# Word transposes through transfers into float32r tiles, in a hybrid attention and retention block

## The chip, the cores and the metric

The kernel runs on one core of a Trainium2 chip. The metric is the device time of one execution in microseconds; of several runs the median counts. A profile is one more execution of the same program, recorded instruction by instruction. Its engines are PE (TensorE; its weight loads are listed apart as PEld), DVE (VectorE), ACT (ScalarE), POOL (GpSimd) and SP (SyncE, which here issues nearly all DMA transfers).

## The reference

One decoder block on `x` of 512 tokens and 1024 channels, all in float32:

```python
h = rms_norm(x, norm_pre)
proj = h @ w_in                       # 6936 columns, split into 15 parts
# mixer A: 8 query heads of 64, 2 key/value groups
#   compressed branch: blocks of 32 tokens, stride 16, through a small MLP -> 31 keys and values
#   selected branch and window branch: at 512 tokens both cover all earlier tokens
o = g0 * o_c + g1 * o_s + g2 * o_w    # g = sigmoid(g_n + b), one per head and branch
y_a = (o * silu(z_n)) @ w_nsa_o
# mixer B: retention, 4 heads, key width 128, value width 256, chunks of 128 tokens
att = einsum(q_chunk, k_chunk) * decay_mask
o = att @ v_chunk + (q_chunk * q_dec) @ R_prev      # R: state carried from chunk to chunk
y_b = (group_norm(o) * silu(z_r)) @ w_ret_o
merged = sigmoid(m_a) * y_a + sigmoid(m_b) * y_b
return x + rms_norm(merged @ w_out, norm_post)
```

There are at most 16 selected blocks of 64 tokens and only 8 blocks in 512 tokens, so the selection leaves no block out.

## The kernel before

**Two types of four bytes.** `FT` is float32, `FR` is float32r, a type of the same size on which TensorE makes one pass over rounded operands. To keep float32's precision the kernel splits a word into a rounded high part and a remainder, both FR (`act` or `cp_any` for the high part, `sub_split` for the remainder), and multiplies in three parts: high by high, high by low, low by high (`mm3`). A transpose also runs on TensorE (`tr`, line 226). Of a float32 tile ("a word transpose") it goes against `ident` in float32; the result in PSUM is the whole word, which is split only then. Only the queries are split first and transposed as FR, against `identr`. The type of a tile is that of the arena it lies in, `arena_f` (42 KB a partition) or `arena_r` (70 KB); `at(kb, n, dt)` cuts a tile out by its address.

**Stages.** The weights come as one stream in the order of their use, 512 KB a transfer (two k tiles of 128 x 512), into one of `NR = 4` raw tiles. `splitter` and `split_lo` make `whi` and `wlo` of each half, nine such pairs ahead (`NW = 9`). `main` is the chain of projections on TensorE: A (compressed and selected keys and values), C (window keys and values, gate row), Q, two compression layers, and then the blocks of `PLAN`: Z, MA, ZR 0, QK 0, VR 0, ZR 1, QK 1, VR 1, MB, NO, RO and so on, with the output projection last. Each block fills two accumulators in turn; a tail for each tile (`tail_a`, `tail_c`, `tail_q`, `tail_qk`, `ret`, ...) takes it out of PSUM and goes on with it.

**Where words are transposed.** `tail_a` and `tail_c` rotate the keys, copy them to doubled columns on DVE (`doubled`, line 511) and transpose them (`keysT`, two transposes a tile; the raw keys and values of the compressed branch, four more). `att_cmp` computes the compressed branch's probabilities and transposes eight tiles of them for each query tile. `att_head` makes the probabilities of one head: two matmuls, mask and maximum on DVE (line 790), exponential on ACT, scaling by gate / sum on DVE or ACT, whichever the planner expects to be done first. `att_block` transposes one key block of the four heads of a group (four transposes to a PSUM bank), splits it into `ph` and `pl` (a `PHL` tile) and adds its product with the values to the group's output bank with two matmuls of 512 columns (`av`). `att_sum` ends a group of a query tile; when all eight are done, it loads the retention's mask `dm` and hands tiles and banks on to retention. `tail_qk` transposes retention's rotated queries and keys (four a tile), `ret` the gated, normalised outputs (four a tile). The norm's row (`rs`) and the compression layers' hidden tiles are transposed as well.

**Buffers.** Rings hand out tiles: `PR` 8 probability tiles (four heads a unit), `PHL` 3, `NAT` 4 tiles of 512 words for tails, `KD6` and `KD2` the doubled keys, `GB` 2, `VR` retention's values, `SMC` 1 for the compressed branch.

**What sets the order.** The class `Order` is a planner: all tails and stages are generators, it runs them against a model of each engine's time, and writes each engine's instructions in the order in which it let them go. `main` has the lowest rank (`MAIN = 9`), attention heads 3, their units 2, most tails 1. So each engine's queue, SP's included, is fixed when the program is built; on the chip an instruction waits for its semaphores, and what stands behind it on its engine waits too. The planner charges a float32 transpose 107 ns and an FR one 58, and 100 and 85 ns for going into float32 on TensorE and back:

```python
    def tr(ps, a, idn, r=0.0):
        T.transpose(ps, a, idn)
        return od.pe(58 if a.dtype == FR else 107, r, a.dtype == FT)
```

Dependencies that decide around the change: `ret` may take the first value tiles out of their accumulators when the attention of query tiles 2 and 3 is done and there is a `VR` tile, the later ones and all further steps when all attention is done; block QK 1 needs the outputs of the first half of retention; NO waits for `ga_split`, which waits for all of retention; RO needs `gbh` and `gbl`, written at the end of `ret`.

Of the kernel before, what the change touches and what calls it, by code (L numbers as in the profile page):

```python
# [27 lines left out]
NR, NW = 4, 9  # L28
# [109 lines left out]
def block_kernel(ctx: ExitStack, tc, x, xT, g_pre, ws, small, w2s, norm_post, rope_r, dmask, out):  # L138
# [5 lines left out]
    cp.tile([P, 48], FT, name="pad")  # L144
# [3 lines left out]
    rp = ctx.enter_context(tc.tile_pool(name="raw", bufs=1))  # L148
    pp = ctx.enter_context(tc.tile_pool(name="ps", bufs=1, space=PSUM))
# [83 lines left out]

    def sub_split(lo, src, hi, r, e="dve"):
        return tt(lo, src, f(hi), OP.subtract, r, e)
# [18 lines left out]
    PHL = Ring([at(o, 1024, FR) for o in (60, 64, 40)])  # L254
# [20 lines left out]
    KD6 = Ring([at(32 + 3 * i, 768) for i in range(2)])  # L275
    KD2 = Ring([at(8 + i, 256) for i in range(2)])
    NAT = Ring([bp.tile([P, 512], FT, name=f"nat{i}") for i in range(4)])
    PR = Ring([at(8 + 2 * i, 512) for i in range(8)])
# [4 lines left out]
    GB = Ring([at(16 + 2 * i, 512) for i in range(2)])  # L283
# [195 lines left out]
    gate = cp.tile([P, NT, 24], FT, name="gate")  # L479
    kc = cp.tile([P, 2, 2, 32], FR, name="kc")  # L480
    vcs = cp.tile([96, 2, 2, 64], FR, name="vcs")
# [26 lines left out]
    def doubled(kn, a, b, kd, r):  # L508

        n = (b - a) // 64  # L510
        V.tensor_copy(kd.rearrange("p (a r c) -> p a r c", a=n, r=2),  # L511
                      kn[:, a:b].rearrange("p (a c) -> p a c", c=64).unsqueeze(2).broadcast_to([P, n, 2, 64]))
        return od.op("dve", 0.53 * n * P + 70, r, True)

    def keysT(kd, off, br, t, r):
        ps = yield from PT.get()
        yield r + PE_LAG
        for g in range(2):
            e = tr(ps[:, g * P:(g + 1) * P], kd[:, off + g * P:off + (g + 1) * P], ident, r)
# [16 lines left out]
    def tail_a(t, ps, e, ring):  # L536
# [8 lines left out]
        kd = yield from KD6.get()  # L545
        e = doubled(kn, 0, 384, kd, e)
        ev = vals(kn[:, 384:512], 0, t, 0.0)
        NAT.put(kn, ev)
        yield from keysT(kd, 512, 0, t, e)
        pc = yield from PT.get()  # L550
        yield e + PE_LAG
        for i in range(4):
            ep = tr(pc[:, i * P:(i + 1) * P], kd[:, i * P:(i + 1) * P], ident, e)
        KD6.put(kd, ep)
# [13 lines left out]
    def tail_c(t, ps, e):  # L568
# [7 lines left out]
        kd = yield from KD2.get()  # L576
        e = doubled(kn, 0, 128, kd, e)
        ev = vals(kn[:, 128:256], 1, t, 0.0)
        NAT.put(kn, ev)
        e = yield from keysT(kd, 0, 1, t, e)  # L580
        KD2.put(kd, e)
# [139 lines left out]
    def av(t, g, st, mv, r):  # L721
        a = avs[t, g]
        e = mm(a["po"], st, mv, a["n"] == 0, a["n"] == a["total"] - 1, r)
        a["n"] += 1
        a["e"] = e
        return e

    def att_cmp(t):
# [5 lines left out]
        for h in range(8):  # L734
# [21 lines left out]
               zc.unsqueeze(2).unsqueeze(3).broadcast_to([P, 8, 3, 32]), OP.mult, e)  # L756
        for g in range(2):
# [3 lines left out]
            for j in range(4):  # L761
                ep = tr(pt[0:96, j * P:(j + 1) * P], s3[:, g * 4 + j, :], ident, e)
            if g == 1:
                SMC.put((sm, s3), ep)
# [7 lines left out]
            ep = av(t, g, vcs[:, g].rearrange("p s c -> p (s c)"), pc, ep)  # L772
            PC.put(pc, ep)

    def att_head(t, g, brs, j, slot):
# [25 lines left out]
        if max(od.eng["act"], e) + (0.833 * L + 186) * nb + 190 < max(od.eng["dve"], e) + (0.521 * L + 191) * nb:  # L801
# [7 lines left out]
        slot["pv"], slot["r"] = pv, e  # L809

    def att_block(t, g, br, b, kt, slots, lastblk):
        r = max(s["r"] for s in slots)
        yield lambda: "po" in avs[t, g]
        yield r + PE_LAG
        pt = yield from PT.get()
        for j in range(4):
            e = tr(pt[:, j * P:(j + 1) * P], slots[j]["pv"][:, b, kt * P:(kt + 1) * P], ident, r)
        if lastblk:
            for s in slots:
                PR.put(s["P"], e)  # L820
# [364 lines left out]
    def main():  # L1185
# [34 lines left out]
        for name, i in PLAN:  # L1220
            if name in ("NO", "RO"):
                blk = Block(4 if name == "NO" else 8, 512)
                xh, xl = (gah, gal) if name == "NO" else (gbh, gbl)
                if name == "NO":
                    yield od.need("ga")
# [154 lines left out]
```

## Time and profile before

| | |
|---|---|
| median of 3 runs | 531.25 us (531.12 to 532.12) |
| profiled execution | 531.09 us, span 529.2 us |
| PE busy | 518.8 us, 98% of the span |
| DVE busy | 390.4 us, 74% |
| ACT busy | 256.5 us, 48% |
| DMA queue of SP | 54.46 MB, 30.4% of 16 engines' span |
| granted TensorE clock | 0.998 |

The span runs from the first to the last instruction; the profiled execution's own time is 1.9 us longer. A busy share is an average over stages. Matmuls overlap in the pipeline, so the cost of one is read from the start of one to the start of the next, not from its duration. In rows with helpers a line is the helper's: 189 is `act`, 201 is `tt`, 210 is `ts`, 222 is `mm`, 226 is `tr`.

### The profile page before, as it was taken

How to read it: one execution, taken by the hardware profiler on the slowest of the kernel's cores; microseconds unless marked ns; L12 is line 12 of the kernel's file. 1: busy time of each engine (PE TensorE's matmuls, PEld its weight loads, DVE VectorE, ACT ScalarE, POOL GpSimd, SP SyncE). 2: the span in 40 equal slices, each digit the busy share in tenths (PEclk: the TensorE clock that was granted, in tenths of full speed). 3: DMA queues.
4: the chain of work that ended last, by engine and by line, in shares of the span. 5: the costliest groups of instructions: out<-in, count | busy, mean ns of one | idle time of the engine just before them, and what ended most of it. 6: DMA issues, size and time to landing. Idle time of an engine off the chain costs nothing.

```text
span 529.2 us, 7325 instructions
## 1 busy us (share of the span) xinstructions
PE 518.8 (98%) x2636; PEld 436.1 (82%) x2636; DVE 390.4 (74%) x924; ACT 256.5 (48%) x552; POOL 12.9 (2%) x32
## 2 busy tenths in 40 slices
PE   8998999999999999999999999999999999999995
PEld 7896888888788888888888888888888888888885
DVE  6799799899999989997777886777737235345533
ACT  6673589448365785483546253525304224123411
POOL 1000000000000000000010000000000000000000
PEclk9999999999999999999999999999999999999999
DMA  8931127401304013123401441131814033305022
GB/s 327 382 121 54 46 66 239 175 1 40 121 1 130 31 40 117 43 84 115 146 35 41 139 142 58 41 120 40 311 48 159 18 142 125 115 1 159 1 98 101
DMA packets 18131, 55.18 MB, mean 104 GB/s; under 512 B 2096, under 2 KB 3120, under 8 KB 18096
## 3 DMA queue, kind: packets, MB, share of 16 engines
q1 hardware_dynamic: 17808, 54.46, 30.4%
q8 instruction: 20, 0.33, 0.3%
q10 hardware_dynamic: 288, 0.27, 0.2%
q14 instruction: 15, 0.12, 0.1%
HBM read 52.63 MB, written 2.10 MB: 103 GB/s over the span
## 4 chain that ended last, share of the span: by engine, by line
PE 84%; DVE 11%; issue 2%; ACT 2%; DMA 1%; DVEq 0%; POOLq 0%; POOL 0%; ACTq 0%
PE bank L222 79%; PE bank L226 5%; DVE arena_f L201 3%; DVE wlo L201 3%; DVE arena_r L201 2%; DVE arena_f L790 1%; DMA raw<-in_stream_dram 1%; DVE nat L201 1%; ACT arena_r L189 1%; ACT whi L189 1%; DVE arena_f L511 1%; DVE arena_f L210 0%; DVE arena_f L214 0%; ACT nat L189 0%; ACT arena_f L189 0%
## 5 line engine op out<-in xcount | busy, mean ns | idle before, releaser
L189 ACT ACTIVATE whi<-raw 128x512 fp32r<-128x512 f32 x151 | 91.9, 628 | 51.4 <-PE bank L222 42.0
L201 DVE TENSOR_TENSOR wlo<-raw,whi 128x512 fp32r<-128x512 f32 x160 | 102.9, 686 | 3.9 <-ACT whi L189 3.3
L222 PE MATMUL bank<-whi,hTh 128*128 128x512 f32 x256 | 99.4, 404 | 0.9 <-ACT whi L189 0.9
L222 PE MATMUL bank<-wlo,hTh 128*128 128x512 f32 x256 | 96.3, 391 | 0.1
L222 PE MATMUL bank<-whi,hTl 128*128 128x512 f32 x256 | 96.3, 391 | 0.0
L222 PE MATMUL bank<-arena_r 128*128 128x256 f32 (+2 forms) x328 | 70.3, 335 | 0.0
L189 ACT ACTIVATE arena_r<-bank 128x512 fp32r<-128x512 f32 (+2 forms) x80 | 45.1, 570 | 46.5 <-PE bank L226 46.3
L222 PE MATMUL bank<-hTh,whi 128*128 128x512 f32 x160 | 63.4, 396 | 0.0
L222 PE MATMUL bank<-hTh,wlo 128*128 128x512 f32 x160 | 62.6, 391 | 0.2 <-DVE wlo L201 0.2
L222 PE MATMUL bank<-hTl,whi 128*128 128x512 f32 x160 | 62.5, 390 | 0.0
L222 PE MATMUL bank<-arena_r,whi 128*128 128x512 f32 x192 | 59.2, 389 | 0.0
L222 PEld LDWEIGHTS bank<-whi,hTl 128*128 128x128 f32 x256 | 48.1, 188 | 10.5
L222 PEld LDWEIGHTS bank<-arena_r 128*128 128x128 f32 x328 | 50.8, 190 | 6.3 <-DVE stat L790 0.3
L222 PEld LDWEIGHTS bank<-whi,hTh 128*128 128x128 f32 x256 | 48.0, 188 | 9.2 <-ACT whi L189 1.0
L222 PEld LDWEIGHTS bank<-wlo,hTh 128*128 128x128 f32 x256 | 48.2, 188 | 9.0 <-DVE wlo L201 0.5
L201 DVE TENSOR_TENSOR arena_r<-bank,arena_r 128x512 fp32r<-128x512 f32 (+2 forms) x72 | 46.9, 656 | 8.3 <-ACT arena_r L189 7.6
L222 PE MATMUL bank<-whi,arena_r 128*128 128x512 f32 (+1 forms) x176 | 49.0, 353 | 0.0
L222 PEld LDWEIGHTS bank<-arena_r,whi 128*128 128x128 f32 x192 | 36.0, 188 | 7.6 <-DVE sg L214 0.2
L189 ACT ACTIVATE arena_f<-arena_f,stat 128x512 f32<-128x512 f32 (+3 forms) x64 | 35.3, 555 | 11.3 <-DVE stat L790 11.2
L226 PE MATMUL bank<-ident,arena_f 128*128 128x128 f32 (+1 forms) x260 | 38.5, 274 | 1.6 <-DVE arena_f L511 1.0
L226 PEld LDWEIGHTS bank<-ident,arena_f 128*128 128x128 f32 (+1 forms) x260 | 31.0, 138 | 9.9 <-DVE arena_f L511 1.5
L222 PE MATMUL bank<-arena_r,wlo 128*128 128x512 f32 x96 | 37.3, 389 | 0.0
(117 smaller groups left out, 669.6 us busy)
## 6 DMA issues: line engine op xcount, KB each, us to landing
raw<-in_stream_dram SPq DMA_DIRECT2D x79, 512.0 KB, 4.1
arena_f<-in_x_dram SPq DMA_DIRECT2D x8, 512.0 KB, 6.9
arena_f<-in_xT_dram SPq DMA_DIRECT2D x8, 256.0 KB, 5.8
arena_f<-in_rope_r_dram SPq DMA_DIRECT2D x8, 256.0 KB, 2.5
out_dram<-arena_f SPq DMA_DIRECT2D x6, 256.0 KB, 2.0
raw<-in_stream_dram SPq DMA_DIRECT2D x4, 280.0 KB, 7.1
arena_f<-in_norm_post_dram SPq DMA_DIRECT2D x1, 512.0 KB, 7.9
out_dram<-arena_f SPq DMA_DIRECT2D x2, 192.0 KB, 1.9
```

The source lines that it names most:

```text
L189: S.activation(o, i, func, **kw)
L201: (V if e == "dve" else G).tensor_tensor(o, a, b, op=op)
L222: T.matmul(ps, a, b, start=start, stop=stop)
L226: T.transpose(ps, a, idn)
L511: V.tensor_copy(kd.rearrange("p (a r c) -> p a r c", a=n, r=2), kn[:, a:b].rearrange("p (a c) -> p a c", c=64).unsqueeze(2).broadcast_to([ ...
L790: V.tensor_tensor_reduce(pv[:, b, :], sv[:, b, :], maskp[:, 512 - L:512], 1.0, -NEG, OP.add, OP.min, nm[:, b:b + 1])
```

## The change

1. A word tile that is to be transposed is first copied by a DMA transfer on SP, from SBUF to SBUF, into a tile of type FR (`moved`; the bits stay as they are), and transposed from there against `identr` (`trs`). This holds for `keysT` and `tail_a`, `att_cmp`, the attention heads, `tail_qk` and `ret`. The norm's row and the hidden tiles of the compression layers stay float32. `doubled` becomes two transfers that write the keys twice; the copy on DVE goes.
2. Attention works in units of two heads instead of four. A head's probabilities go from their `PR` tile (5 instead of 8) to one of 8 FR tiles (`PF`). A group of transposes is two key blocks of two heads instead of one block of four, and `av` adds half an output bank at a time (256 columns). The choice of the engine for the scaling is moved by 590 ns towards ACT.
3. Memory is regrouped: 3 raw tiles instead of 4; `PHL` 2 tiles instead of 3, one of which `att_cmp` borrows for its transfer (one `att_cmp` at a time, ring `ONE`); six 2 KB tiles serve as `PF` in attention and, after `regroup`, as `NAT` and as `RF` (the FR tiles of `ret`'s transfer). The mask `dm` is loaded by `regroup`.
4. `ga_split` waits for the last uses of the tiles it overwrites (`used10` to `used13`) instead of all of retention, its remainder part is spawned apart, and the loads that stood behind it wait in `late_loads`.

```diff
-NR, NW = 4, 9
+NR, NW = 3, 9
...
+    def moved(dst, src, r):
+
+        DMA.dma_start(f(dst), src)
+        return od.dma(P * size(dst) * 4, r)
+
+    def trs(ps, a, r=0.0):
+        return tr(ps.bitcast(FR), a, identr, r)
...
-    PHL = Ring([at(o, 1024, FR) for o in (60, 64, 40)])
+    PHL = Ring([at(o, 1024, FR) for o in (60, 64)])
...
-    NAT = Ring([bp.tile([P, 512], FT, name=f"nat{i}") for i in range(4)])
-    PR = Ring([at(8 + 2 * i, 512) for i in range(8)])
+    pf = [flex(f"pf{i}", FR) for i in range(6)]
+    PF = Ring(pf + [at(40, 512, FR), at(42, 512, FR)])
+    RF = Ring([])
...
+    lent = [at(18 + 2 * i, 512) for i in range(3)]
+    NAT = Ring([bp.tile([P, 512], FT, name="nat0")] + lent)
+    PR = Ring([at(8 + 2 * i, 512) for i in range(5)])
...
-    def doubled(kn, a, b, kd, r):
-
-        n = (b - a) // 64
-        V.tensor_copy(kd.rearrange("p (a r c) -> p a r c", a=n, r=2),
-                      kn[:, a:b].rearrange("p (a c) -> p a c", c=64).unsqueeze(2).broadcast_to([P, n, 2, 64]))
-        return od.op("dve", 0.53 * n * P + 70, r, True)
+    def doubled(dst, src, r):
+
+        n = src.shape[-1] // 64
+        for i in range(2):
+            DMA.dma_start(f(dst).rearrange("p (a r c) -> p a r c", a=n, r=2)[:, :, i, :],
+                          src.rearrange("p (a c) -> p a c", a=n))
+        return od.dma(P * size(dst) * 4, r, 2)
...
+        turn = yield from ONE.get()
+        phl = yield from PHL.get()
+        cf = phl[:, 0:768]
+        e = moved(cf, s3.rearrange("p h c -> p (h c)"), e)
...
-        if max(od.eng["act"], e) + (0.833 * L + 186) * nb + 190 < max(od.eng["dve"], e) + (0.521 * L + 191) * nb:
+        if max(od.eng["act"], e) + (0.833 * L + 186) * nb < max(od.eng["dve"], e) + (0.521 * L + 191) * nb + 400:
...
-        slot["pv"], slot["r"] = pv, e
+        wf = slot["F"][:, 0:nb * L]
+        slot["r"] = moved(wf, Pj[:, 0:nb * L], e)
+        slot["pv"] = wf.rearrange("p (b c) -> p b c", b=nb)
+        PR.put(Pj, slot["r"])
...
+        for br, kt in blocks:
+            for j in (2 * p, 2 * p + 1):
+                s = slots[br, j]
+                e = trs(pt[:, n:n + P], s["pv"][:, br - s["b0"], kt * P:(kt + 1) * P], r)
+                n += P
...
+        for i, (br, kt) in enumerate(blocks):
+            vs = VS[:, kt, br, g].rearrange("p s c -> p (s c)")
+            for v in (ph, pl):
+                ep = av(t, g, p, vs, v[:, i * 256:(i + 1) * 256], e)
+        PHL.put(phl, ep)
...
+    def regroup():
+
+        got = []
+        for _ in range(len(pf) + 2):
+            got.append((yield from PF.get()))
+        for i in range(len(lent)):
+            NAT.put(flex(f"nat{i + 1}"))
+        for b in pf[len(lent):]:
+            RF.put(b)
+        od.flags.add("state")
...
+        DMA.dma_start(dm, dmask.rearrange("h p c -> p h c"))
+        dmr.append(od.dma(P * 2048))
...
+        wf = qk_l[t]
+        e = moved(wf, t1, e)
...
+        wf = yield from RF.get()
+        e = moved(wf, gb, e)
...
     def ga_split():
-        yield od.need(*RETA)
+        yield od.need("used10", "used11")
```

More of the change, by code (lines that the diff above doesn't have):

```diff
@@ L274, in block_kernel, with flex @@
     Xv = at(28, 1024).rearrange("p (l g c) -> p l g c", l=16, g=2)
-    KD6 = Ring([at(32 + 3 * i, 768) for i in range(2)])
-    KD2 = Ring([at(8 + i, 256) for i in range(2)])
-    NAT = Ring([bp.tile([P, 512], FT, name=f"nat{i}") for i in range(4)])
-    PR = Ring([at(8 + 2 * i, 512) for i in range(8)])
+    KD6 = Ring([at(62 + 3 * i, 768, FR) for i in range(2)])
+    KD2 = Ring([at(40 + i, 256, FR) for i in range(4)])
+    def flex(name, dt=FT):
+        return bp.tile([P, 512], dt, name=name, tag="flex", bufs=6)
+    pf = [flex(f"pf{i}", FR) for i in range(6)]
+    PF = Ring(pf + [at(40, 512, FR), at(42, 512, FR)])
+    RF = Ring([])
+    ONE = Ring(["only one part of the compressed branch at a time holds such a buffer"])
+    lent = [at(18 + 2 * i, 512) for i in range(3)]
+    NAT = Ring([bp.tile([P, 512], FT, name="nat0")] + lent)
+    PR = Ring([at(8 + 2 * i, 512) for i in range(5)])
     SMC = Ring([(at(27, 256).rearrange("p (h c) -> p h c", h=8), at(24, 768).rearrange("p (h c) -> p h c", h=8))])
@@ L282, in block_kernel @@
     kf = [at(38 + t, 256) for t in range(NT)]
-    GB = Ring([at(16 + 2 * i, 512) for i in range(2)])
+    GB = Ring([])
     AM = Ring([at(24 + i, 256) for i in range(2)])
@@ L478, in block_kernel @@
     bg = cst[:, NT * 32:NT * 32 + 24]
[L479 to L481 removed]
+    kc = ep.tile([P, 2, 2, 32], FR, name="kc")
+    vcs = ep.tile([96, 2, 2, 64], FR, name="vcs")
+    gate = ep.tile([P, NT, 24], FT, name="gate")
     pes = [cst[:, NT * 32 + 24 + 16 * i:NT * 32 + 40 + 16 * i] for i in range(2)]
@@ L518, in keysT @@
         for g in range(2):
-            e = tr(ps[:, g * P:(g + 1) * P], kd[:, off + g * P:off + (g + 1) * P], ident, r)
+            e = trs(ps[:, g * P:(g + 1) * P], wf[:, off + g * P:off + (g + 1) * P], r)
         yield e, "act"
@@ L544, in tail_a @@
         e = rope16(v, t, (2, 2), e)
-        kd = yield from KD6.get()
-        e = doubled(kn, 0, 384, kd, e)
+        wf = yield from KD6.get()
+        e = doubled(wf, kn[:, 0:384], e)
         ev = vals(kn[:, 384:512], 0, t, 0.0)
-        NAT.put(kn, ev)
-        yield from keysT(kd, 512, 0, t, e)
+        NAT.put(kn, max(e, ev))
+        yield from keysT(wf, 512, 0, t, e)
         pc = yield from PT.get()
@@ L771, in att_cmp @@
             yield ep + PE_LAG
-            ep = av(t, g, vcs[:, g].rearrange("p s c -> p (s c)"), pc, ep)
+            for p in range(2):
+                e2 = av(t, g, p, vcs[:, g].rearrange("p s c -> p (s c)"), pc[:, p * 256:(p + 1) * 256], ep)
+            ep = e2
             PC.put(pc, ep)
@@ L890, in att_sum @@
                 PS.put(b)
+    def regroup():
[7 more added lines that the diff above has]
+        od.flags.add("state")
+        left = list(lent)
+        while left:
+            b = yield from NAT.get()
+            if any(b is q for q in left):
+                left = [q for q in left if q is not b]
+            else:
+                NAT.put(b)
+                yield od.now + 500.0
+        DMA.dma_start(dm, dmask.rearrange("h p c -> p h c"))
+        dmr.append(od.dma(P * 2048))
+        for i in range(2):
+            GB.put(at(16 + 2 * i, 512))
     ATT = tuple(f"att{t}{g}" for t in range(NT) for g in range(2))
@@ L1008, in ret @@
         eo = e
+        usedr[t] = e
+        od.flags.add(f"used{hp}{t}")
         if t < NT - 1:
@@ L1056, in ret_state @@
     def ret_state(hp, t, pr, e):
+        yield od.need("state")
         yield e, "act"
```

121 lines of the change are left out of this document (69 added, 52 removed).

## The prediction

> **What bounds the kernel now.** I read the page's head and its chain of waits first: which engine fills the span, and does the chain agree?
>
> ```profile
> span 529.2 us, 7325 instructions
> PE 518.8 (98%) x2636; PEld 436.1 (82%) x2636; DVE 390.4 (74%) x924; ACT 256.5 (48%) x552; POOL 12.9 (2%) x32
> PE 84%; DVE 11%; issue 2%; ACT 2%; DMA 1%; DVEq 0%; POOLq 0%; POOL 0%; ACTq 0%
> ```
>
> TensorE is busy for 518.8 of 529.2 us and makes 84% of the chain. An average can hide stages with another limit, so the second view was the busy time by stretch, cut at the block borders: start, first projection, key/value tails, attention, retention, tail.
>
> ```profile
> 0.00:6.00 6.00, 3.79 (x17) 3.60 (x18) 2.13 (x4) 2.84 (x4) 2.51 (x15) 1.00 0.73 229
> 6.00:27.00 21.00, 21.00 (x93) 17.38 (x94) 16.06 (x33) 15.88 (x29) 1.02 (x1) 1.00 0.99 386
> 27.00:60.00 33.00, 31.18 (x196) 26.52 (x194) 30.06 (x95) 16.95 (x46) 0.94 (x4) 1.00 0.26 86
> 60.00:256.00 196.00, 195.63 (x1043) 163.90 (x1041) 178.32 (x476) 124.28 (x295) 0.00 (x0) 1.00 0.25 81
> 256.00:370.00 114.00, 114.00 (x598) 97.14 (x597) 88.49 (x196) 51.62 (x100) 6.26 (x8) 1.00 0.28 88
> 520.00:529.20 9.20, 3.25 (x28) 3.04 (x26) 3.23 (x8) 0.95 (x4) 0.54 (x1) 0.88 0.30 114
> ```
>
> The columns are the stretch, its length, then PE, PEld, DVE, ACT and POOL busy, the granted clock and DMA. PE's idle time lies in the start (2.2 us), the last output rows (6.0), 1.8 from 27 to 60, and 0.4 in the 196 us of attention. So almost every microsecond of PE work taken away shortens the program, and what is only hidden elsewhere is worth nothing. But from 27 to 256 VectorE is busy for 208 of 229 us: a second limit, 9% behind. A 512-column matmul costs PE 21.00 / 93 = 0.226 us (second row).
>
> **The transposes, which is what PE gains.** The answer for the transpose helper's line says how many there are, and when:
>
> ```profile
> L226 PE MATMUL bank<-ident,arena_f x260: 270/272/331, 29.6 to 365.5; 128*128 128x128 f32 x114, 128*96 128x128 f32 x16
> L226 PE MATMUL bank<-identr,arena_r x32: 222/245/253, 58.5 to 84.3; 128*128 128x128 f32 x32
> L226 PE MATMUL bank<-ident,nat x32: 270/272/273, 215.9 to 321.1; 128*128 128x128 f32 x32
> L226 PE MATMUL bank<-ident,rs x4: 272/272/294, 50.6 to 50.9; 128*128 128x128 f32 x4
> ```
>
> Long-type transposes: 260 + 32 + 4. The change leaves the gate row (4) and the two hidden layers' (2 x 2, in line 226's first row). It makes 288 short: 16 in `keysT` in pairs, the other 272 in 68 groups of four. Their number stays. The `identr` row is the new kind, already there for the queries, and so the price needs no guess. Durations overlap in the pipe; the price is read from start to start over a group and the matmul behind it, minus two plain matmuls. First long, then short:
>
> ```profile
> 227.54 0.39 PE L222 MATMUL bank<-whi,hTl 128*128 128x512 f32 x1
> 227.78 0.60 PE L226 MATMUL bank<-ident,nat 128*128 128x128 f32 x4
> 228.13 0.48 PE L222 MATMUL bank<-whi,hTh 128*128 128x512 f32 x1
> 228.45 0.39 PE L222 MATMUL bank<-wlo,hTh 128*128 128x512 f32 x1
> ```
>
> ```profile
> 59.40 0.40 PE L222 MATMUL bank<-whi,hTl 128*128 128x512 f32 x1
> 59.63 0.46 PE L226 MATMUL bank<-identr,arena_r 128*128 128x128 f32 x4
> 59.93 0.46 PE L222 MATMUL bank<-whi,hTh 128*128 128x512 f32 x1
> 60.23 0.40 PE L222 MATMUL bank<-wlo,hTh 128*128 128x512 f32 x1
> ```
>
> Long: 228.45 - 227.54 - 0.452 = 0.458 us. Short: 60.23 - 59.40 - 0.452 = 0.378. The matmul behind either starts its successor late (0.32 and 0.30 instead of 0.226), so leaving a group costs nearly the same in both. Difference 0.080 us, 0.06 to 0.10 with the rounding and the spread of single starts. 68 x 0.080 = **5.4 us off PE** (4.1 to 6.8). For the eight pairs, less than half a group each, I take nothing. The gain is 1% and not more because a short group is far from a quarter of a long one. Per group the planner's own table claims much more (4 x (107 - 58) ns and two mode changes of 100 and 85 ns: 0.38 us); the rows do not bear that out.
>
> The Trainium skill, "TensorE: Matmul & The Clock Gate", section "Weight-path perf modes", speaks against the change: loading 128 columns of weights takes some 107 ns, and the fast load is not for FP32. If four-byte short words count as FP32, a transpose stays bound by its weights at 107 ns and the term would be 0 instead of 5.4. The short group's row above, 0.378 us for four with the way out, already lies below 4 x 107.
>
> **What PE has more.** Units of two heads: a group is now two key blocks x two heads instead of one block x four. Groups stay 40 (four head pairs x (1 + 2 + 3 + 4) now; 10 blocks x 2 branches x 2 key groups before), and so do their evictions. But value matmuls are four of 256 columns instead of two of 512, with
>
> ```profile
> 83.41 0.28 PE L222 MATMUL bank<-whi,arena_r 128*128 128x256 f32 x1
> ...
> 83.89 0.28 PE L222 MATMUL bank<-whi,arena_r 128*128 128x256 f32 x1
> ```
>
> four starts in 0.48 us: 0.120 each. 40 x (4 x 0.120 - 2 x 0.226) = 1.1, and eight compressed-branch matmuls halved, 8 x 0.014 = 0.1: **1.2 us more**. Net 4.2 us less PE work, 2.9 to 5.6.
>
> **What VectorE loses and ScalarE gets.**
>
> ```profile
> L511 DVE COPY arena_f<-nat x8: 286/427/561, 28.7 to 56.4; 128x768 f32<-128x768 f32 x4, 128x256 f32<-128x256 f32 x4
> L210 DVE TENSOR_SCALAR arena_f<-arena_f,stat,gate x64: 339/448/551, 64.4 to 248.5; 128x512 f32<-128x512 f32 x16, 128x384 f32<-128x384 f32 x16, 128x256 f32<-128x256 f32 x16, 128x128 f32<-128x128 f32 x16
> PE bank L226 <- DVE arena_f L511: 1.0, 2, 0.6
> ```
>
> Eight doubling copies go: 8 x 0.427 = 3.4 us of VectorE between 28 and 57, where PE waited for two of them. All 64 softmax scalings sit on VectorE now (64 x 0.448 = 28.7 us). The new test moves the choice 590 ns towards ScalarE; between 0 and 28.7 us leave, a tiny product each coming back. ScalarE is busy for 124 of 196 us there, so it is mostly free at that point, and I expect more than half to go. Direct value on PE: nothing while PE is the limit. It is cover.
>
> **What the transfers add, and their waits.** SP issues 16 (doubling, two per tile) + 4 (compressed branch) + 48 (head tiles) + 8 + 8 (retention) = 84 transfers, some 18 MB, a third of the bytes of
>
> ```profile
> q1 hardware_dynamic: 17808, 54.46, 30.4%
> out_dram<-arena_f SPq DMA_DIRECT2D x6, 256.0 KB, 2.0
> arena_f<-in_rope_r_dram SPq DMA_DIRECT2D x8, 256.0 KB, 2.5
> SPq L315 <- DVE wlo L201: 381.3, 70, 24.8
> ```
>
> so the share of the queues goes to some 40%. On-chip copies do not occur in this trace; the nearest are 256 KB in 2.0 (out) and 2.5 us (in). I take 2.5 behind each word tile; upper bound 5, with a weight load ahead in the queue. What hides it:
>
> Heads and groups work with these steps (mask, exponential; eviction, remainder), the largest shape of each:
>
> ```profile
> L790 DVE CUSTOM_DVE_ANT_0 arena_f<-bank,maskp 128x512 f32<-128x512 f32 x16 | 10.8, 686 | 0.0
> L189 ACT ACTIVATE arena_f<-arena_f,stat 128x512 f32<-128x512 f32 x16 | 11.4, 717 | 3.2 <-DVE stat L790 3.1
> L189 ACT ACTIVATE arena_r<-bank 128x512 fp32r<-128x512 f32 x64 | 37.3, 591 | 30.4 <-PE bank L226 30.2
> L201 DVE TENSOR_TENSOR arena_r<-bank,arena_r 128x512 fp32r<-128x512 f32 x56 | 38.1, 686 | 7.5 <-ACT arena_r L189 7.2
> ```
>
> Heads. 48 head tiles pass in 184 us (64.4 to 248.5, the scalings' row), 3.8 us each. Five probability tiles may be held 19 us each and eight short tiles 31. A tile's own way, 0.69 + 0.72 + 0.55 and a transfer of 2.5, is 4.5 us, 10 with queueing. Cost 0; if nothing covered it, 2.5 us would repeat at the eight turns of query tile and key group: 20 us.
>
> Key tails. A second lies between them and their transposes, while projections C and Q give PE 34 us of work; the 3.4 us of copies go in exchange. Between -1.8 (all idle time from 27 to 60 gone) and +2: I take 0.
>
> Retention. The transfers stand behind the rotation and the gated norm, both in the background; its mask load now waits for a regrouping of buffers. The last of its transposes and the first matmul of NO are
>
> ```profile
> 365.16 0.60 PE L226 MATMUL bank<-ident,arena_f 128*128 128x128 f32 x4
> 370.41 0.62 PE L222 MATMUL bank<-arena_r,whi 128*128 128x512 f32 x2
> ```
>
> and RO, which needs them, comes 48 matmuls (11 us) after the second: 16 us of cover against 2.5 to 5. Cost 0.
>
> SP is in order: behind a transfer that waits for VectorE or ScalarE stand weight loads. They already wait up to 24.8 us without PE noticing (0.4 us idle in attention), since nine split halves, 9 x 12 x 0.226 = 24 us of matmuls, lie ready. One raw tile less (three) shortens the lead by 5.4 us; at the start the queues are 0.99 full until 27, and a load issued one or two microseconds later lands no later. Cost 0.
>
> The earlier split before NO replaces no wait: PE is busy for 114.00 of 114.00 us up to there.
>
> **Sum.** 531.09 us (profiled execution; span 529.2 and 1.9 around it) - 5.4 + 1.2 = 526.9. The median of the runs is 0.16 higher: **527.0 us**; own range 525.5 to 528.3.
>
> **Rivals.** (1) *More*: with VectorE relieved the 1.8 us from 27 to 60 close too, and groups save 0.10: 531.25 - 5.6 - 1.8 = 523.9; for it the two waits for the copies, against it the transfer in the same place. (2) *VectorE holds attention*: the last of attention ends where it did, the projections arrive some 3 us sooner at VR0, whose evictions wait for it, and stand. The three rows show how tight that is:
>
> ```profile
> 255.79 0.57 PE L222 MATMUL bank<-arena_r 128*128 128x256 f32 x4
> 256.02 0.69 DVE L201 TENSOR_TENSOR arena_f<-nat,arena_f 64x512 f32<-64x512 f32 x1
> 256.39 0.43 SPq L884 DMA_DIRECT2D arena_f<-in_dmask_dram x1
> ```
>
> (retention's first products, the last attention sum, the mask load: within 0.6 us). 56 of the 68 groups lie before; 56/68 of 4.2 is lost, 530.5. Against it the scalings that leave. (3) *Slower, by the two PHL tiles* (three before). A group holds one from eviction to its value matmuls, and the compressed branch now borrows one for its transfer until an output bank comes free. With one left, 40 groups in 184 us allow a hold of 4.6 us; eviction, remainder and four matmuls need 0.59 + 0.69 + 0.48 = 1.8 unqueued. From 4.6 us on it decides: a hold of 5.4 in 10 of the groups costs 8 us, the gain off: 531.25 + 8 - 4.2 = 535. (4) *Slower, by SP's order*: transfers wait long enough to eat the 24 us lead; one such stall of a landing and a split, some 5 us by the rows above, less the gain: 532. (5) The weights bind the short transposes as the long ones: only the 1.2 is left, 532.4. This is the skill's rule above; the short row contradicts it. That the matmul side stays as it is for another reason is the same case.
>
> **Chances.** Forecast 0.54, (1) 0.16, (2) 0.12, (3) 0.10, (4) 0.05, (5) 0.03. A difference under 0.2% (1.1 us) can't be told from none: faster 0.70, same 0.12, slower 0.18. The range, 522.8 to 533.0, takes in (1), (2), (4) and (5) and leaves out most of (3).
>
> On (4), the Trainium skill, "DMA: Bandwidth & Descriptors", section "Anatomy of one DMA", puts any semaphore wait on the issuing sequencer before dispatch; the SP row of 381.3 us of waits agrees, and no row here shows a transfer between two loads.
>
> **What would show it.** Right: PE busy some 4 us less, its idle time from 27 to 256 still near 2 us; 320 `identr` transposes, eight `ident` ones, starts of groups as in the short rows; no copies; fewer than 32 scalings on VectorE. Wrong: PE idle before 256 (2); idle with ACT or PE waiting for the PHL tiles (3); `whi` waiting for raw tiles after 60 us (4); groups still 0.46 (5).

## The result: 538.6 us, 1.4% slower

The changed kernel takes 538.55 us (median of four runs, 538.0 to 543.97), the kernel before 531.68 (four runs, 531.12 to 533.35): ratio 1.0144, 95% interval 1.0113 to 1.0176. Predicted were 527.0 us and a range to 533.0; the time lies above it. The profiled execution is the one of 543.97 us, at a granted clock of 0.991 where the other three had 0.994 to 0.996, so what is read from it may be more than the other three paid.

First the page's head and its chain, as they were read for the kernel before:

```profile
span 542.2 us, 7782 instructions
PE 520.3 (96%) x2724; PEld 440.1 (81%) x2724; DVE 378.5 (70%) x914; ACT 270.9 (50%) x589; POOL 12.9 (2%) x32
PE 79%; DMA 8%; DVE 8%; ACT 2%; issue 2%; POOLq 0%; DVEq 0%; POOL 0%; ACTq 0%; SPq 0%
```

DMA has gone from 1% to 8% of the chain: transfers now stand between two pieces of matmul work. The span is 13.0 us longer: PE is idle for 11.5 us more, and its busy time has grown by 1.5 (518.8 to 520.3) where the sum has it fall by 4.2. Three rows of the busy time by stretch say where (same columns as before: stretch, length, PE, PEld, DVE, ACT, POOL, granted clock, DMA share, GB/s):

```profile
27.00:60.00 33.00, 30.56 (x193) 26.48 (x192) 27.88 (x88) 16.61 (x43) 0.96 (x4) 1.00 0.58 152
60.00:256.00 196.00, 188.05 (x1088) 161.34 (x1087) 163.56 (x465) 138.66 (x332) 0.00 (x0) 0.98 0.44 148
256.00:370.00 114.00, 111.86 (x589) 94.44 (x588) 85.09 (x188) 49.12 (x94) 5.20 (x7) 1.00 0.33 107
```

TensorE stands for 7.95 us in the attention stretch (60 to 256) where it stood for 0.37, and for 2.1 us in retention where it never stood. VectorE has 14.8 us less to do in attention, so it isn't VectorE over the stretch as a whole. The granted clock in attention is 0.98 instead of 1.00. What PE waited for (total, times, longest):

```profile
PE bank L227 <- DMA arena_r<-arena_f: 4.0, 3, 1.8
PE bank L227 <- DMA pf<-arena_f: 3.3, 3, 1.6
PE bank L227 <- DMA arena_r<-nat: 2.0, 2, 1.4
PE bank L227 <- ACT rsrow L190: 1.8, 1, 1.8
```

The first three rows are the new transfers: eight waits, 9.3 us. Line 227 is the transpose behind the transfer. By their tiles and times, 2.3 us lie at two head tiles of attention (0.75 at 92.8 and 1.59 at 105.1 us), 3.2 at the compressed branch (the rows of 128*96), and 3.8 in retention: 2.0 behind `tail_qk`'s transfers from `nat`, 1.8 behind `ret`'s, where the tiles named `pf` are `RF` tiles by then. The eight awaited transfers landed 2.6 to 5.4 us after their issue, five of them after 4.7 or more. Four of the waits, both at the compressed branch and the longer of each pair in retention (start, duration, instruction, and in brackets the idle time before it and its releaser):

```profile
126.23 0.58 PE L227 MATMUL bank<-identr,arena_r 128*96 128x128 f32 x4 [1.82 <-DMA arena_r<-arena_f]
188.07 0.48 PE L227 MATMUL bank<-identr,arena_r 128*96 128x128 f32 x4 [1.39 <-DMA arena_r<-arena_f]
330.17 0.53 PE L227 MATMUL bank<-identr,arena_r 128*128 128x128 f32 x4 [1.37 <-DMA arena_r<-nat]
389.11 0.53 PE L227 MATMUL bank<-identr,pf 128*128 128x128 f32 x4 [0.99 <-DMA pf<-arena_f]
```

Here is the second wait at a head tile, on SP's and on PE's timeline:

```profile
97.21 2.27 SPq L334 DMA_DIRECT2D raw<-in_stream_dram  x2
99.57 0.47 SPq L237 DMA_DIRECT2D pf<-arena_f  x1
```

```profile
102.44 0.50 PE L223 MATMUL bank<-hTh,wlo 128*128 128x512 f32 x1 [1.08 <-DVE wlo L202]
...
105.05 0.46 PE L227 MATMUL bank<-identr,pf 128*128 128x128 f32 x3 [1.59 <-DMA pf<-arena_f]
105.35 0.47 PE L223 MATMUL bank<-hTh,whi 128*128 128x512 f32 x1
...
106.28 0.63 PE L223 MATMUL bank<-hTh,whi 128*128 128x512 f32 x1
106.71 0.63 PE L223 MATMUL bank<-hTl,whi 128*128 128x512 f32 x1
```

SP issued two weight loads (the second at about 99.1) and a word transfer behind them at 99.57; PE could go on only at 105.05, 5.5 us after the issue. PE executes the order that the planner wrote, so all the matmuls behind that transpose stood too; the rows behind it show no wait of their own.

The sum's own rows came as predicted: 320 short transposes (168 + 152), eight long ones, and no copies on VectorE.

```profile
L227 PE MATMUL bank<-identr,arena_r x168: 221/244/309, 34.5 to 335.5; 128*128 128x128 f32 x136, 128*96 128x128 f32 x32
L227 PE MATMUL bank<-identr,pf x152: 220/245/283, 74.0 to 389.4; 128*128 128x128 f32 x152
L227 PE MATMUL bank<-ident,rs x4: 272/273/294, 51.5 to 51.9; 128*128 128x128 f32 x4
L227 PE MATMUL bank<-ident,arena_f x4: 270/271/277, 87.8 to 98.3; 128*128 128x128 f32 x4
```

```profile
232.53 0.39 PE L223 MATMUL bank<-whi,hTl 128*128 128x512 f32 x1
232.76 0.46 PE L227 MATMUL bank<-identr,arena_r 128*128 128x128 f32 x4
233.06 0.47 PE L223 MATMUL bank<-whi,hTh 128*128 128x512 f32 x1
233.36 0.40 PE L223 MATMUL bank<-wlo,hTh 128*128 128x512 f32 x1
```

Starts of a group: 233.36 - 232.53 - 0.452 = 0.378 us, the predicted price.

### The profile page after: what moved, and what is told of

The parts are those of the page before. It is cut to its first block, busy times and chain, and to the rows that moved or that the text cites. A ratio compares the mean times of both kernels' runs of the same rounds, so it can differ in the third digit from the quotient of the medians.

```text
span 542.2 us, 7782 instructions
## 1 busy us (share of the span) xinstructions
PE 520.3 (96%) x2724; PEld 440.1 (81%) x2724; DVE 378.5 (70%) x914; ACT 270.9 (50%) x589; POOL 12.9 (2%) x32
## 3 DMA queue, kind: packets, MB, share of 16 engines
q1 hardware_dynamic: 36048, 72.82, 40.2%
## 4 chain that ended last, share of the span: by engine, by line
PE 79%; DMA 8%; DVE 8%; ACT 2%; issue 2%; POOLq 0%; DVEq 0%; POOL 0%; ACTq 0%; SPq 0%
PE bank L223 75%; PE bank L227 4%; DMA pf<-arena_f 3%; DMA arena_r<-nat 3%; DVE wlo L202 2%; DVE arena_f L202 2%; DMA arena_r<-arena_f 2%; DVE arena_r L202 1%; ACT arena_f L190 1%; DMA raw<-in_stream_dram 1%; ACT whi L190 1%; DVE arena_f L820 1%; ACT arena_r L190 0%; DVE arena_f L215 0%; DVE nat L202 0%
## 5 line engine op out<-in xcount | busy, mean ns | idle before, releaser
L190 ACT ACTIVATE whi<-raw 128x512 fp32r<-128x512 f32 x142 | 84.8, 627 | 56.8 <-PE bank L223 36.7
L202 DVE TENSOR_TENSOR wlo<-raw,whi 128x512 fp32r<-128x512 f32 x160 | 104.0, 687 | 10.0 <-ACT whi L190 9.6
L223 PE MATMUL bank<-arena_r 128*128 128x256 f32 (+3 forms) x408 | 73.7, 306 | 0.5 <-DVE arena_r L202 0.5
L223 PEld LDWEIGHTS bank<-arena_r 128*128 128x128 f32 x408 | 60.4, 192 | 5.7 <-DVE arena_r L202 0.7
L190 ACT ACTIVATE arena_f<-arena_f,stat 128x384 f32<-128x384 f32 (+3 forms) x110 | 58.6, 557 | 8.0 <-DVE stat L202 4.4
L202 DVE TENSOR_TENSOR arena_r<-bank,arena_r 128x512 fp32r<-128x512 f32 (+2 forms) x72 | 47.0, 657 | 18.4 <-ACT arena_r L190 17.7
L223 PEld LDWEIGHTS bank<-hTh,wlo 128*128 128x128 f32 x160 | 30.5, 190 | 8.2 <-DVE wlo L202 1.5
L223 PEld LDWEIGHTS bank<-whi,arena_r 128*128 128x128 f32 x176 | 32.1, 189 | 4.6
```

Of the source, the lines that this page charges most:

```text
L190: S.activation(o, i, func, **kw)
L202: (V if e == "dve" else G).tensor_tensor(o, a, b, op=op)
L223: T.matmul(ps, a, b, start=start, stop=stop)
```

## The experiments

Each ratio is against the kernel before, timed in the same series on the same chip (medians there 531.6 to 532.8 us). Differences between two edited kernels are of medians; where the two come from different series, 1.2 us of them can be the series'.

**Later landings in the plan (e1).** The planner takes each new transfer to land 2.5 us later; so it places the transposes later in PE's order. The work stays; all engines' orders are planned anew.

```diff
 def moved: ...
-        return od.dma(P * size(dst) * 4, r)
+        return od.dma(P * size(dst) * 4, r) + 2500.0
 def doubled: ...
-        return od.dma(P * size(dst) * 4, r, 2)
+        return od.dma(P * size(dst) * 4, r, 2) + 2500.0
```

> Edit: only the planner's estimate of when a word tile's transfer has landed is 2.5 us later (both in moved and in doubled); the same work, the same tiles, the same transfers. PE's instructions come in another order: each transpose stands further back in PE's queue. Theory P (places): the transposes stand in PE's fixed order at a landing that the transfers miss by 1 to 3 us, and PE stands still with all that is behind them; then the stops go, and the time falls from 538.5 to 525 to 530 us, below the kernel before (531.5). Theory B (buffers): five probability tiles, two PHL tiles and eight short tiles are too few for the transfer's latency; then tiles are held still longer and the time stays at 538 or grows. Theory S (scalings and VectorE): the transfers don't matter; no change, 538 within 1 us.

Measured: 532.41 us (10 runs, 530.03 to 534.6), ratio 1.0001 (0.9975 to 1.0026): 6.1 us less than the changed kernel, but 5.4 over the forecast of 527.0 and above the 525 to 530 that the theory of places expected. Its profiled execution took 530.11 us. PE's waits and two stretches:

```profile
PE bank L223 <- DVE wlo L202: 1.9, 4, 1.0
PE bank L227 <- ACT rsrow L190: 1.8, 1, 1.8
...
PE bank L223 <- DVE nat L215: 1.2, 1, 1.2
```

```profile
60.00:256.00 196.00, 193.87 (x1143) 167.20 (x1141) 168.18 (x471) 144.92 (x340) 0.00 (x0) 1.00 0.43 151
256.00:370.00 114.00, 112.44 (x589) 95.23 (x588) 86.37 (x194) 50.28 (x98) 6.58 (x8) 1.00 0.34 110
sum 528.10, PE 513.85 PEld 436.84 DVE 375.85 ACT 274.00 POOL 14.01; mean PE 73.41 PEld 62.41 DVE 53.69 ACT 39.14 POOL 2.00
```

No wait for a transfer is left. PE is busy for 513.85 us, 5.0 less than before. But it still stands for 2.1 us in attention and 1.6 in retention, where one product waits 1.2 us for VectorE (`nat`).

**The same order, long transposes (e2).** The transposes of the moved tiles are done as float32 ones; the order of instructions stays that of the changed kernel.

```diff
 def trs(ps, a, r=0.0):
-        return tr(ps.bitcast(FR), a, identr, r)
+        T.transpose(ps, f(a), ident)
+        return od.pe(58, r, False)
```

> Edit: the changed kernel with its order left as it is, but each transpose of a transferred tile is done in float32 against ident, read from the same short tile. It takes away the change's gain on PE and keeps its transfers and waits. If the 0.080 us per group of four of the prediction hold and PE has no free time in which to hide it, 68 groups cost 5.4 us more: 544 us. If PE's stops take part of it up (PE waits anyway), 2 to 4 us more: 540.5 to 542.5. If short transposes gain nothing (bound by their weights), no change: 538.5.

Measured: 542.14 us (541.8 to 544.19), ratio 1.018 (1.0144 to 1.0215): 3.6 us over the changed kernel. A part of the term falls into stops, which longer transposes merely fill: PE's waits for the transfers come to 5.9 us in its profile, and to 9.3 in the changed kernel's.

**The kernel before with three raw tiles (e3).**

```diff
-NR, NW = 4, 9
+NR, NW = 3, 9
```

> Edit: the kernel before with three raw tiles instead of four, nothing else. The prediction costed this at 0: 531.5 within 1 us. In the profile of the changed kernel the first projection's 96 matmuls take 23.7 us instead of 21.7; if the missing raw tile is the cause, 533 to 534 here; if it is TensorE's clock in that one execution, no change.

Measured: 536.56 us (535.87 to 538.71), ratio 1.0082 (1.0053 to 1.0111), 4.5 us more, above the 533 to 534 expected if the raw tile costs. ScalarE, which splits the weights, now waits for raw tiles 21 times instead of 9:

```profile
ACT whi L189 <- DMA raw<-in_stream_dram: 27.6, 21, 3.1
```

(before: 6.4 us.) The planner makes a new order for three tiles, so this is the raw tile and the order that follows from it. What a new order alone can cost is seen in e9.

**Transfers on ScalarE's queue (e4).**

```diff
 def moved(dst, src, r):
-        DMA.dma_start(f(dst), src)
+        S.dma_start(f(dst), src)
```

> Edit: the 68 transfers of moved are issued by ScalarE's queue instead of SP's, at the same point of the program; weight loads stay on SP's queue. Theory F (in front): a transfer takes 4 to 5.6 us instead of 2.2 when a 512 KB weight load stands in front of it in the one queue; then the long landings go to 3 us or less, and the waits of PE for them shrink: 532 to 536 us, if ScalarE doesn't lose as much by standing before each issue (68 x 0.45 us of issuing, and its waits for VectorE). If the 16 DMA engines are shared all the same, landings stay at 4 to 5 us and the time at 538 or, with ScalarE's loss, above 540.

Measured: 548.09 us (547.7 to 550.99), ratio 1.0295 (1.0255 to 1.0335). Sorting the 84 transfers of each trace (64 to 384 KB; the 16 doublings stay on SP here) by whether a weight load was under way at the issue, the median from issue to landing is 2.23 us without and 3.6 us with one (28 transfers, 11 of them over 4 us, the longest 5.6) in the changed kernel, and 2.23 and 3.9 here (30, 14 over 4 us). A queue of their own doesn't shorten them. PE's waits for transfers come to 12.2 us instead of 9.3; that ScalarE loses by standing at them itself was expected, and isn't shown apart.

**Four raw tiles again (e5); with later landings (e6); with corrected prices as well (e7).** The 4 KB per partition of the raw tile come from one pair of split weights. Corrected prices: the planner counts a short transpose 58 ns, where the rows give 0.378 / 4.

```diff
-NR, NW = 3, 9
+NR, NW = 4, 8
```

```diff
 e6, e7: + 2500.0 in moved and doubled, as in e1
 e7 also, in tr and in Order.pe:
-        return od.pe(58 if a.dtype == FR else 107, r, a.dtype == FT)
+        return od.pe(94 if a.dtype == FR else 110, r, a.dtype == FT)
-            cost += 100.0 if exact else 85.0
+            cost += 10.0 if exact else 10.0
```

> The changed kernel with four raw tiles again; the 4 KB per partition come from the split weights (eight pairs of tiles instead of nine). Nothing else is edited; the written-out order is planned anew. Theory (three terms: -4 us on the matmul engine, +4.5 us for the raw tile, +6 us for landings that the order sets too early): the middle term goes, 534 us (532.5 to 535.5), and the waits of PE for transfers stay at some 9 us. Rival one: the raw tile cost 4.5 us only in the kernel before, here PE already stands for other reasons while raw tiles are late: 537.5 to 539. Rival two: the ninth pair of weight tiles is worth as much as the fourth raw tile: 537.5 to 540, with PE waiting on wlo more than now.

> Four raw tiles and eight weight pairs, and the order planned as if every new transfer landed 2.5 us later than it does now (only the order of PE's instructions changes with this). Theory: both losing terms go and the -4 us of PE stay: 528 us (527 to 529), faster than both kernels. Rival: the later order and the raw tile give the same waits back, so that they do not add: 530 to 532.

> As the one before, and the planner's prices for transposes set to what the trace shows (a short one 94 ns, a float32 one 110, a change of kind 10). Theory: with right prices the plan's clock no longer runs ahead of PE (it ran 24 us ahead by 387 us in the changed kernel), landings need less luck: 526 to 528. Rival: the margin already covers it, and the prices change nothing: within 1 us of the run with the margin alone.

Measured: e5 531.61 us, ratio 0.9996 (0.9977 to 1.0014); e6 540.51, 1.0172 (1.0147 to 1.0197); e7 530.77, 0.9983 (0.9968 to 0.9999). None fits its number. e5 wins 6.9 us and not 4.5; its order, planned without any margin, has only one wait for a transfer left:

```profile
PE bank L227 <- DMA arena_r<-nat: 0.4, 1, 0.4
```

e6, which should have had both gains, is the slower by 8.9 us: by its order PE stands elsewhere, and in two of its stretches the granted clock falls.

```profile
PE bank L223 <- DVE arena_r L215: 3.0, 1, 3.0
```

```profile
27.00:60.00 33.00, 29.09 (x179) 25.30 (x178) 26.14 (x83) 14.79 (x39) 0.96 (x4) 0.95 0.55 150
256.00:370.00 114.00, 108.43 (x567) 91.55 (x566) 85.21 (x188) 48.86 (x95) 5.20 (x7) 0.97 0.33 110
```

So the theory of three terms that add falls. Between these two neighbours, a margin of 2.5 us apart, the order that the planner happens to write makes 9 us.

**Long transposes in the later order (e8).** e1 with the edit of e2.

> The changed kernel with the later order (three raw tiles; 532.4 us), with the same transposes of the same short-type tiles done as float32 ones again, in the same order of instructions. It measures the term of the sum by itself, in a kernel whose PE does not stand at the transfers: 68 groups of four by 0.080 us. Theory: the whole 5.4 us come back, 537.8 us (536.8 to 538.5). Rival: even there PE's stops take in a part, as they did in the changed kernel (3.6 us): 536 or less.

Measured: 537.25 us (535.7 to 539.28), 4.85 us over e1, and 5.4 when each is set against the kernel before of its own series (5.7 and 0.3 us over it): within the expected range. PE is busy for 6.0 us more in the two profiles (519.85 and 513.85 us).

**The planner's prices alone: in the kernel before (e9) and in the changed one (e10); prices and margin with three raw tiles (e11).** Edits as in e7.

> The kernel before, its order planned with the prices that the trace shows for transposes (float32 110 ns, short 94, a change of kind 10). A control for the later runs: how much does another order alone move a kernel that has none of the new transfers? Theory: the matmul engine of the kernel before stands for only 2 us between 27 and 520 us, so a better order can win at most that: 530 to 532. Rival: the planner's prices held the kernel before back as well, and the changed kernel's best orders owe their times to the prices: 526 to 529.

> The changed kernel with the same three prices corrected and nothing else: three raw tiles, landings planned as in the changed kernel. Theory one (landings: the plan counts on a transfer sooner than it lands when a weight load is in front of it): the waits of PE for transfers stay at 5 us or more, 535 to 539. Theory two (prices: a group of short transposes is planned at 232 ns and takes 378, the plan runs ahead of PE and its places no longer fit): the waits go without any margin, 530 to 532.5.

> The changed kernel (three raw tiles, nine weight pairs) with the later landings and the corrected prices. Its neighbour with four raw tiles and eight weight pairs took 530.8 us. Theory one (the raw tile costs 4.5 us in this kernel as it did in the kernel before): 534 to 536. Theory two (with this order the raw tile is worth no more than the ninth weight pair): 530 to 532.

Measured: e9 534.52 us, ratio 1.0045 (1.0026 to 1.0063); e10 534.89, 1.0052 (1.0031 to 1.0073); e11 532.55, 0.9997 (0.9975 to 1.0019). e9, outside both expectations: with no change to its work the kernel before is 0.45% slower in another order, in which one wait alone takes 3.3 us, and the granted clock from 27 to 60 is 0.95:

```profile
PE bank L226 <- ACT rsrow L189: 3.3, 1, 3.3
```

e10: the waits for transfers are down from 9.3 us to two of 0.9 and 0.5, as theory two has it, but the time is only 3.7 us lower and misses its number; PE stands for others instead.

```profile
PE bank L223 <- DVE arena_r L202: 1.5, 1, 1.5
...
PE bank L227 <- DMA pf<-arena_f: 0.9, 1, 0.9
...
PE bank L227 <- DMA arena_r<-nat: 0.5, 1, 0.5
```

e11, 0.5 us above theory two's range, against e7: 0.14% between ratios whose intervals overlap. With this order the fourth raw tile, paid with a weight pair, can't be told from none.

**The order that its own plan ends soonest (e12), and its transposes long (e15).** Of several settings of tiles, margin and look-ahead this is the one whose plan is shortest: NR, NW = 4, 8; a margin of 800; SLACK 1200 instead of 700; prices of e7. e15 is e12 with the edit of e2.

> Four raw tiles, eight weight pairs, corrected prices, landings planned 0.8 us later, and the planner looks 1.2 us ahead instead of 0.7: of the orders tried on paper this one ends its own plan soonest. Theory: plan and chip keep the distance that they have in the neighbour with 2.5 us (9 us), 528 to 530, faster than the kernel before. Rival: 0.8 us are too few behind a weight load (those transfers land 1.4 us and more after the free ones), the waits for transfers return: 532 to 536.

> The best kernel so far (529.1 us) with the same transposes of the same tiles done as float32 ones, in the same order of instructions. If the term of the sum is what makes it faster than the kernel before: 4.9 us (as with the later order) to 5.4 us more, 534 to 534.5. If its gain comes from the order: 531 or less.

Measured: e12 529.1 us (527.72 to 530.43), ratio 0.993 (0.9903 to 0.9957), faster than both kernels. Three of its stretches and the sum:

```profile
60.00:100.00 40.00, 39.21 (x252) 34.07 (x252) 36.67 (x100) 34.29 (x75) 0.00 (x0) 1.00 0.60 207
100.00:256.00 156.00, 155.06 (x899) 133.43 (x898) 136.26 (x390) 106.57 (x262) 0.72 (x1) 1.00 0.39 135
256.00:370.00 114.00, 113.63 (x590) 96.22 (x589) 87.74 (x191) 51.76 (x99) 6.48 (x7) 1.00 0.35 114
sum 527.20, PE 513.94 PEld 436.78 DVE 378.45 ACT 270.46 POOL 13.90; mean PE 64.24 PEld 54.60 DVE 47.31 ACT 33.81 POOL 1.74
```

1.7 us of stops in attention instead of 7.95. Against the kernel before of its series e12 saves 3.7 us, most of the 4.2 that the sum promised. Three waits for transfers are left, 3.2 us, 2.9 of them at the key tails: from 27 to 60 PE stands for 3.4 us. e15: 532.27 us (531.8 to 535.26), ratio 1.001 (0.9994 to 1.0026), 3.2 us over e12 (3.4 against the kernels before of their series), between the two expectations. PE's busy time differs by 4.8 us in the two profiles (518.74 in e15, below, and 513.94), the spans by 3.4: longer transposes fill 1.4 us of stops.

```profile
0.00:530.60 530.60, 518.74 (x2724) 441.97 (x2724) 378.42 (x916) 270.42 (x587) 13.90 (x32) 1.00 0.41 139
```

Without the short transposes the same order only equals the kernel before: the gain is theirs.

**Word transfers on GpSimd's queue (e13: e10 with it; e14: four raw tiles, eight pairs, prices and look-ahead of e12).** In e10 SP stood for up to 12.8 us at one word transfer not yet scaled, with the weight loads of the hidden layers behind it.

```diff
 def moved(dst, src, r):
-        DMA.dma_start(f(dst), src)
-        return od.dma(P * size(dst) * 4, r)
+        G.dma_start(f(dst), src)
+        return od.op("pool", 1000, r) + 2600.0
```

> The changed kernel with three raw tiles, nine weight pairs and corrected prices, and the 68 transfers of words issued on GpSimd's queue instead of SP's (planned as 1 us of GpSimd and 2.6 us to the landing). Its neighbour with SP's queue took 534.9 us; between 60 and 100 us PE stood for 2.8 us in it, while SP stood up to 12.8 us in front of a word transfer whose words were not scaled yet, with the weight loads of the hidden layers behind it. Theory one (SP's order): the weight loads are no longer held, PE stands for less than 1 us between 60 and 100 us, 530 to 532.5. Theory two (the stretch is bound by the transfers' own time among the weight loads, whoever issues them): the stands stay within 0.5 us of the neighbour's, 534 to 536. On ScalarE's queue the same transfers cost 9.5 us, since ScalarE then stood itself; GpSimd is busy for 13 us in all.

> The best kernel so far (four raw tiles, eight weight pairs, corrected prices, 1.2 us of look-ahead, 529.1 us) with the word transfers on GpSimd's queue. Theory one (SP's order costs): 526.5 to 528.5. Theory two (it does not, with four raw tiles): 529 to 531.

Measured: e13 533.79 us, ratio 1.0036 (1.0016 to 1.0057); e14 531.87, 0.999 (0.9976 to 1.0004). In e13 PE stands for 2.81 us between 60 and 100, as long as in e10 (2.80), 2.1 of them for a transfer that landed late and 0.7 for weights; that is theory two, though the time lies a little under its range:

```profile
PE bank L227 <- DMA arena_r<-arena_f: 2.1, 1, 2.1
```

e14 is 2.8 us slower than its neighbour with SP's queue, above the range of either theory. So with the transfers out of SP's order one kernel is 1.1 us faster than its neighbour by the medians and the other 2.8 slower; both edits also made a new plan, and what SP's order costs is not measured apart.

## Why the prediction was wrong

**PE's term: right.** The short group costs 0.378 us as read. Undone, it gives back 4.85 us (e8), 3.6 (e2) and 3.2 (e15) of the 5.4, or 5.4, 3.2 and 3.4 against the kernels before of their series. The size holds where PE doesn't stand (PE's busy time falls by 5.0 us from the kernel before to e1, net of what the 256-column matmuls add, against the predicted net of 4.2); elsewhere a part is lost to stops. Rival (5), long and short bound alike by their weights, falls with e8. The Trainium skill's rule that was weighed there ("TensorE: Matmul & The Clock Gate", "Weight-path perf modes") doesn't reach these words: read so that they count as FP32, it would have had no gain.

**"Heads ... Cost 0" and "Retention ... Cost 0": the steps that failed.** The sum put the waits for the transfers at nothing; in the profile they are 9.3 us, 2.3 at head tiles, 3.8 in retention and 3.2 at the compressed branch, for whose four transfers the sum had no term at all. The transfer's length was about right, 2.3 us in the median and up to 5.6, where 2.5 and a bound of 5 were taken:

```profile
pf<-arena_f SPq DMA_DIRECT2D x26, 256.0 KB, 2.3
```

What failed is the thought that room on average covers a late landing. PE's order is fixed ahead, and a transpose placed in it before its transfer has landed stops all of PE, whatever the buffers hold on average. In the order that leaves more room (e1) these waits are gone, and the time is 6.1 us lower. That the 2.5 us of margin did it is not separated from the new order: with corrected prices and no margin 1.4 us of them are left (e10), and in e5's order, with neither, 0.4. So the trace shows the waits and where they lie; why this plan ran into them and e5's didn't stays open. The upper bound of 5 us was in the text, but it was set against the cover and not against the place in PE's order. The key tails, also costed at 0, have none of the waits in this order, but two, 2.9 us, in that of e12.

**PE's busy time: a loss that the sum had no term for.** It grew by 1.5 us where 4.2 less were forecast, 5.7 us apart. In this execution two stretches of 3.4 us ran at half the granted clock behind stops, which costs 1.7 us each, and at the start PE made 84 matmuls from 6 to 27 us instead of 93, some 2.0 us: 5.4 us (the rows are in the last section). How much of this is in the median isn't known: one execution was profiled.

**"SP is in order ... three raw tiles: Cost 0": doubtful in the kernel before, not settled in the changed one.** In e3 the tile costs 4.5 us together with its new order; a new order alone cost 0.45% in e9 (1.8 us by the medians). The lead of nine halves x 12 x 0.226 us holds where a half feeds 12 wide matmuls; in the hidden layers it feeds matmuls of 256 columns at 0.120 us, so the lead is shorter there. In the changed kernel the tile can't be told from none once the order has margin (e11, e7), and freeing the weight loads from the word transfers on SP changed the time by -1.1 us (e13 against e10) and +2.8 (e14 against e12), with new plans both times.

**"VectorE: 208 of 229 us", rival (2): right mechanism, wrong place.** In attention as a whole VectorE has got room (163.56 of 196). But finer stretches show it full in the hidden layers, before the change as after. The kernel before, then e1:

```profile
70.00:90.00 20.00, 20.00 (x142) 18.05 (x141) 19.71 (x47) 19.14 (x42) 0.00 (x0) 1.00 0.50 166
```

```profile
70.00:90.00 20.00, 18.12 (x130) 15.85 (x129) 19.27 (x53) 19.11 (x43) 0.00 (x0) 1.00 0.69 237
```

VectorE and ScalarE, which split the weights, are busy for 19 of 20 us in both; PE kept up without a stop, and in e1 stands for 1.9 us, 1.7 of it for `wlo`. By this reading PE work taken away in such a stretch is not time. My cut at block borders hid it. This reading was not tested by a run of its own. The scalings went as the step had it: 46 of 64 to ScalarE.

**What else the sum lacked: a new order.** The sum took the old order with shorter pieces. Any edit makes the planner write another, and the old one was a good one: PE stood for 2.2 us in 343 us. e9 pays 0.45% for a new order alone; e5 and e6, one margin apart, differ by 8.9 us. That is a part of why e1, without waits for transfers, comes to 532.4 and not to 527. Against the kernel before, its PE stands for 1.0 us more from 27 to 60, 1.8 more in attention (the stretch above) and 1.6 more in retention, 4.4 us. From 27 to 60 the longest wait is one for the norm's row (`rsrow`, 1.8 us), which the kernel before doesn't have; in retention it is the one for `nat` (1.2). Why the order puts them there was not tested; the stops change place from order to order. That part stays open, and so do the 2.3 us by which e1's median lies above its profiled execution.

**The other rivals.** (3) The two PHL tiles: e1 and e12 have the same two and lose nothing like the 8 us; no run with three was made. (4) SP's order eats the lead: 532 was nearer to the time than the forecast, and `whi` waits for raw tiles for 18.4 us where it waited for 6.4, but PE waited for weights for only 2 us; the longer waits lay at the transfers themselves. (1) needed a stretch from 27 to 60 without stops; it grew, from 1.8 to 2.4 us. Rightly costed: the group price, the 256-column matmuls, the share of the queues (40.2%), the scalings. A slower kernel had 0.18.

## What to carry to other kernels

In a kernel whose order is planned ahead, a transfer's price is what PE stands at the place where the order has its user, not what the buffers' mean cover leaves: look up the landings with a heavy load in flight, put that into the plan, and look at the waits again. Before a sum of removed work is taken for time, ask how much the order alone is worth here (0.45% and more): a change of 1% in work can be lost in one order and arrive in another, as this one did at 529.1 us. An engine's stops also take part of any saving, so a term is best checked by undoing it in the same order of instructions.

## What the runs showed of the hardware

An on-chip transfer (256 KB the most frequent size) took 2.2 us by itself, and 3.6 in the median and up to 5.6 us with a 512 KB weight load in flight. On ScalarE's queue it was 2.2 and 3.9, so a queue of its own doesn't take the delay away. The Trainium skill, "DMA: Bandwidth & Descriptors", section "Issuing engines are not separate DMA queues", says that transfers of all issuing engines run on the same 16 DMA engines and interleave, and that a second engine saves only the issuing time; e4 agrees. On GpSimd's queue (e13) the median over all is 2.3 us, as on SP's, and the longest 5.1.

The rows from 106.28 us on show something else: after stops of 1.08 and 1.59 us, matmuls start 0.43 us apart instead of 0.226. The granted clock is 0.50 there, and again behind the stop of 1.82 us at 126.23:

```profile
106.00:109.00 3.00, 3.00 (x10) 2.27 (x8) 0.69 (x1) 0.20 (x1) 0.00 (x0) 0.50 0.50 175
127.00:129.00 2.00, 2.00 (x7) 1.71 (x7) 1.11 (x4) 1.04 (x3) 0.00 (x0) 0.50 0.00 0
```

Each of the two lasts 3.4 us and so costs 1.7 us, as much as a stop. The profiles of e4, e6, e7, e9, e10 and e13 have such stretches too, each behind stops of 1.2 to 3.3 us; those of the kernel before and of e1, e2, e3, e5, e8, e11, e12, e14 and e15 have none before the last output rows. Their length alone doesn't decide: the wait of 1.8 us for the norm's row is followed by half the clock in e4 and e6, that of 1.2 us in e10 too, while the same wait of 1.8 us in the changed kernel (at 56 us) and in e1 is not. So a part of what is put down to the order above, in e6 and e9 above all, is the clock's answer to the order's stops.

Starts 0.43 us apart also stand at 6 to 10 us in some profiled executions (the changed kernel's, e5's, e7's) and not in others (the kernel before's, e1's), where the clock's column shows 1.00 in both; that is some 2 us between executions. Whether it changes between executions of one kernel no profile shows. The Trainium skill, "TensorE: Matmul & The Clock Gate", section "HAM oscillation — how this bites in real kernels", names idle gaps above some 3.4 us as the limit; here a stop of 1.82 us, and two of 2.7 us together with three matmuls and a transpose between them, sufficed. When a stop has this price isn't settled by these runs.
